# A hybrid-attention layer: the order of the first stage (loads, first products, squares of x) is changed

## The chip, the core and the metric

The kernel runs on one core of a Trainium2 chip. The metric is the time of one launch on the device, in microseconds, as the median of several runs. The engines are TensorE (PE in the profile; PEld is its weight load), VectorE (DVE), ScalarE (ACT), GpSimd (POOL) and SyncE (SP), which here only issues transfers. An engine takes its instructions in the order of the program, and waits at the first one whose inputs are not there.

## The reference

One decoder layer on 512 tokens of width 1024, all in float32:

```
h    = rms_norm(x, norm_in)
proj = h @ w_in                         # queries, keys, values and gates of two attention groups
a    = sliding-window attention with sinks (8 query heads, 2 key/value heads)
b    = block-sparse attention (8 heads, blocks of 256 keys)
x    = x + concat(a * silu(a_g), b * silu(b_g)) @ w_out
gate = sigmoid(rms_norm(x, ple_norm) @ w_ple_gate)
x    = x + (p @ w_ple_proj) * gate      # p: 512 x 256, w_ple_proj: 256 x 1024
out  = rms_norm(x, final_norm)
```

What matters here is the start: the product of p with w_ple_proj, the squares of x for the first norm, and the first projection (keys and values of the window group, "akv"), for which the normed x has to be transposed.

## The kernel before

Float32 operands are split in two parts, a rounded copy (the hi part, made by ACT, `AF.Copy`) and the rest (the lo part, made by DVE, `tensor_sub`). A product is then three products: hi by hi, lo by hi, hi by lo. `split_T` (L143, L144), `Weights.split` (L116, L118) and `split_ple` write such pairs.

The first stage is one block of the program, written by hand under `manual_schedule()`: every engine and every queue takes its instructions in the order in which the lines stand. It has these parts.

- **Loads.** p comes in four blocks of 128 tokens (`p_sb`), w_ple_proj in two halves of 512 columns with two row blocks each (`wraw_p[:, n, k]`), then x in four blocks (`x_t`), then the weights of akv. Before, SP's queue carries p, x and the second half of w_ple_proj, and ACT's queue the first half and `g_rows` (norm_in, 4 KB). A transfer takes one of eight completion semaphores in turn and waits for the transfer that had it before.
- **Dummy products** (`warm_up(n)`, L193): n products of a block of zeros, with no reader. 21 stand ahead of the first real work and 5 behind the first transposes.
- **p by w_ple_proj.** `p_trans(t)` (L245 to L247) transposes block t of p on PE into PSUM (two transposes), ACT writes the hi part (`pTh`) and DVE the lo part (`pTl`). `ple_mm(t, n, k)` (L283) is three products of 512 columns: hi by hi, lo by hi (`pTl`), hi by lo (`wpl`). There are four blocks t, two halves n and two row blocks k: 48 products. `ple_out` copies a finished bank to SBUF, on ACT ("A") or DVE ("D").
- **Squares and norms of x.** `x_square(t)` makes the sum of squares of block t, block 0 on DVE (L258), the others on ACT (L255); POOL makes the inverse root (L128, L133); `x_norm(t)` (L262, DVE) scales the block in place.
- **Transposes of x and akv.** `x_trans(k)` (L268, L270, L271) transposes column block k of all four blocks of x on PE, and ACT and DVE write the hi and lo parts, `acts`. `akv_mm(k)` (L302) is six products with them. Of the 48 products of p, the last six (block 3, second half) stand around the first transposes of x, before they begin and between the first two.

Everything behind (the projections of 16 weight chunks, both attentions, the output products) is left as it is. There the order comes from a list of pieces that are run between the steps of the attention.

Of the kernel before, what the change touches and what calls it, by code (L numbers as in the profile page):

```python
# [10 lines left out]
F32 = mybir.dt.float32  # L11
BF16 = mybir.dt.bfloat16
F32R = mybir.dt.float32r
AF = mybir.ActivationFunctionType
ALU = mybir.AluOpType

P = 128
# [21 lines left out]
def hybrid_layer_kernel(  # L39
# [130 lines left out]
    with ExitStack() as ph1:  # L170
# [4 lines left out]
        p_sb = cp1.tile([P, NT, PLE], F32, name="p_sb")  # L175
        pv = p.rearrange("l b (t p) d -> p (l b t) d", p=P)
        wraw_p = cp1.tile([P, 2, 2, 512], F32, name="wraw_p")
        nc.sync.dma_start(p_sb[:, 0:1], pv[:, 0:1])
        nc.scalar.dma_start(wraw_p[:, 0, 0], wp[:, 0, 0:512])
        nc.scalar.dma_start(wraw_p[:, 0, 1], wp[:, 1, 0:512])  # L180
        g_rows = cp1.tile([KC, P], F32, name="g_rows")
        nc.scalar.dma_start(g_rows, norm_in.rearrange("l (k c) -> (l k) c", c=P))
        nc.sync.dma_start(p_sb[:, 1:2], pv[:, 1:2])
        nc.sync.dma_start(p_sb[:, 2:4], pv[:, 2:4])
        warm = cp1.tile([P, P], BF16, name="warm")
        nc.vector.memset(warm, 0.0)
        first = cp1.tile([P, 1], F32, name="first")
# [3 lines left out]
        def warm_up(n):  # L191
            for _ in range(n):
                nc.tensor.matmul(accw[:, 0:P], warm[:, 0:P], warm, start=True, stop=True)  # L193
# [2 lines left out]
        g_col = cp1.tile([P, KC], F32, name="g_col")  # L196
        x_sb = [xp.tile([P, D], F32, name="x_t", bufs=NT) for t in range(NT)]
        nc.sync.dma_start(x_sb[0], x2d[0])
        nc.sync.dma_start(wraw_p[:, 1], wp[:, :, 512:1024])
        for t in range(1, NT):  # L200
            nc.sync.dma_start(x_sb[t], x2d[t])
# [59 lines left out]
        def x_norm(t):  # L261
            nc.vector.tensor_scalar_mul(x_sb[t], x_sb[t], rx[t])  # L262
# [17 lines left out]
        def ple_mm(t, n, k, parts=(0, 1, 2)):  # L280

            for j in parts:
                nc.tensor.matmul(pacc[t, n], (pTl if j == 1 else pTh)[:, k, tok(t)],  # L283
                                 (wpl if j == 2 else wph)[:, n, k], start=k == 0 and j == 0, stop=k == 1 and j == 2)
# [8 lines left out]
        def split_ple(n, k):  # L293
            split_T(wph[:, n, k], wpl[:, n, k], wraw_p[:, n, k])
# [10 lines left out]

        lo0 = p_trans(0)
        gp = bank([P, KC], "gp", "o")
        warm_up(5)
        for t in range(NT):
            ple_bank(t, 0)  # L310
        lo0()
        nc.scalar.activation(wph[:, 0, 0], wraw_p[:, 0, 0], AF.Copy)
        p_trans(1)()
        nc.vector.tensor_sub(wpl[:, 0, 0], wraw_p[:, 0, 0], wph[:, 0, 0].bitcast(F32))
        ple_mm(0, 0, 0, (0, 1))
        lo2, lo3 = p_trans(2), p_trans(3)
        nc.tensor.transpose(gp, g_rows, ident[0:KC, 0:KC])
        ple_mm(1, 0, 0, (0, 1))
        ple_mm(0, 0, 0, (2,))
        ple_mm(1, 0, 0, (2,))  # L320
        lo2()
        lo3()
        split_ple(0, 1)
        ple_mm(2, 0, 0)
        ple_mm(3, 0, 0)
        nc.vector.tensor_copy(g_col, gp)
        for t in range(NT):
            ple_mm(t, 0, 1)
        x_square(0, "D")
        split_ple(1, 0)  # L330
        x_norm(0)
        split_ple(1, 1)
        ple_out(0, 0, "A")
        ple_out(1, 0, "D")
        for t in range(3):
            ple_bank(t, 1)
            for k in range(2):
                ple_mm(t, 1, k)
        x_square(1)
        ple_out(2, 0, "D")  # L340
        ple_out(3, 0, "A")
        x_norm(1)
        x_square(2)
        x_norm(2)
        x_square(3)
        x_norm(3)
        ple_bank(3, 1)
        ple_mm(3, 1, 0)
        for m in range(2):
            akv[m] = bank([P, 512], "acc_akv", "S")  # L350
        x_trans(0)
        w_akv.split()
        tables = bias_tables()
        ple_mm(3, 1, 1)
        x_trans(1)
        w_akv.split()
        akv_mm(0)
        ple_out(0, 1, "D")
        ple_out(1, 1, "A")
# [631 lines left out]
```

## Time and profile before

| what | us |
|---|---|
| median of 3 runs | 323.25 (322.18 to 323.43) |
| the profiled execution | 322.3 |
| its span, first to last instruction | 320.6 |
| PE busy | 307.7 (96%) |
| DVE busy | 226.0 (70%) |
| ACT busy | 185.9 (58%) |
| POOL busy | 66.3 (21%) |

The page gives the busy time of each engine over the span; the view by stretches of time gives the same for parts of it. The timeline lists instructions with their start and length, and in brackets how long the engine had nothing to do before and what released it. The chain of waits follows the end back to the start. The profile page gives the granted clock of PE as full (9 of tenths) in all slices but the last one.

### The profile page before, as it was taken

To read this page: it belongs to the slowest core of one execution; us is meant where nothing else is said; L and a number is where in the kernel's file an instruction comes from. 1 tells how busy PE (TensorE), PEld (TensorE's weight loads), DVE (VectorE), ACT (ScalarE), POOL (GpSimd) and SP (SyncE) were. 2 spreads that over 40 slices of the span, in tenths; PEclk is the share of its full clock that TensorE was granted. 3 is DMA by queue.
4 is the path that set the end of the run, shared out by engine and by line. 5 is a ranking of instruction groups with operands and counts; after the bars stand their busy time and mean duration, and the time that the engine had idled before them with its cause. 6 is when DMAs were issued, how large, how long until landed. Compare 5 with 4: busy or idle time off the path is not lost.

```text
span 320.6 us, 4721 instructions
## 1 busy us (share of the span) xinstructions
PE 307.7 (96%) x1641; PEld 259.9 (81%) x1641; DVE 226.0 (70%) x516; ACT 185.9 (58%) x419; POOL 66.3 (21%) x118
## 2 busy tenths in 40 slices
PE   7999999999999999899999999999999999999990
PEld 6878788888889888699888878877888888888890
DVE  2876766886787868878878796859758656672544
ACT  4755656656475648677678676788157323541341
POOL 1240102435434351600003130012300110000011
PEclk9999999999999999999999999999999999999997
DMA  7962598150405072751443403004956700000113
GB/s 234 390 164 83 148 227 232 41 133 1 127 7 177 23 183 76 200 155 40 135 98 120 112 0 133 1 0 116 384 174 246 264 1 0 2 0 0 66 67 131
DMA packets 33224, 37.61 MB, mean 117 GB/s; under 512 B 1432, under 2 KB 24992, under 8 KB 33200
## 3 DMA queue, kind: packets, MB, share of 16 engines
q1 hardware_dynamic: 31952, 33.94, 34.0%
q0 software_dynamic: 800, 2.62, 4.2%
q10 hardware_dynamic: 448, 0.74, 0.7%
q8 instruction: 13, 0.21, 0.3%
q14 instruction: 11, 0.09, 0.1%
HBM read 32.52 MB, written 2.16 MB: 108 GB/s over the span
## 4 chain that ended last, share of the span: by engine, by line
PE 72%; DVE 12%; issue 6%; ACT 4%; POOL 3%; DMA 1%; POOLq 0%; SPq 0%; ACTq 0%; DVEq 0%
PE acc L451 8%; PE acc L452 8%; PE acc L453 8%; PE acc L137 7%; PE acc L139 7%; PE acc L138 7%; PE acc_ple L283 3%; PE acc_akv L302 3%; PE Sb L611 3%; PE accv L137 2%; PE oaccb L641 2%; PE accv L139 2%; PE accv L138 2%; PE tpb L631 2%; DVE q L499 2%
## 5 line engine op out<-in xcount | busy, mean ns | idle before, releaser
L557 ACT ACTIVATE st<-st,nm 128x257 f32<-128x257 f32 (+1 forms) x32 | 15.2, 478 | 22.0 <-DVE nm L554 20.0
L137 PE MATMUL acc<-hi_wg,h 128*128 128x512 f32 (+1 forms) x72 | 26.7, 370 | 0.0
L139 PE MATMUL acc<-hi_wg,h 128*128 128x512 f32 (+1 forms) x72 | 26.4, 367 | 0.0
L451 PE MATMUL acc<-acts,hi_bkq 128*128 128x512 f32 x64 | 26.4, 412 | 0.0
L138 PE MATMUL acc<-lo_wg,h 128*128 128x512 f32 (+1 forms) x72 | 26.3, 365 | 0.0
L451 PE MATMUL acc<-acts,hi_aqg 128*128 128x512 f32 x64 | 26.2, 410 | 0.0
L137 PE MATMUL acc<-hi_wo,acts 128*128 128x512 f32 x64 | 25.4, 397 | 0.5 <-DVE G L529 0.5
L453 PE MATMUL acc<-acts,lo_aqg 128*128 128x512 f32 x64 | 25.2, 393 | 0.0
L453 PE MATMUL acc<-acts,lo_bkq 128*128 128x512 f32 x64 | 25.1, 392 | 0.0
L139 PE MATMUL acc<-hi_wo,acts 128*128 128x512 f32 x64 | 25.1, 392 | 0.0
L452 PE MATMUL acc<-acts,hi_bkq 128*128 128x512 f32 x64 | 25.1, 392 | 0.0
L138 PE MATMUL acc<-lo_wo,acts 128*128 128x512 f32 x64 | 25.1, 392 | 0.0
L452 PE MATMUL acc<-acts,hi_aqg 128*128 128x512 f32 x64 | 25.1, 392 | 0.0
L614 ACT ACTIVATE stb<-stb,nmb 128x128 f32<-128x128 f32 (+3 forms) x32 | 17.8, 558 | 9.0 <-DVE nmb L612 8.7
L582 POOL TENSOR_SCALAR_AFFINE_SELECT pta<-pta 128x512 fp32r<-128x512 f32 x24 | 17.3, 719 | 14.3 <-DVE pta L144 13.2
L137 PE MATMUL accv<-hi_bv,acts 128*128 128x256 f32 x64 | 18.7, 293 | 1.5 <-DVE kt L144 1.5
L536 POOL TENSOR_TENSOR O<-O,sg 128x512 f32<-128x512 f32 x8 | 11.4, 1428 | 39.5 <-DVE sg L535 39.3
L139 PE MATMUL accv<-hi_bv,acts 128*128 128x256 f32 x64 | 18.0, 282 | 0.0
L138 PE MATMUL accv<-lo_bv,acts 128*128 128x256 f32 x64 | 18.0, 281 | 0.0
L839 ACT ACTIVATE sq<-x 128x512 f32<-128x512 f32 x15 | 9.5, 631 | 14.2 <-DVE x L901 11.6
L612 DVE CUSTOM_DVE_ANT_0 stb<-Sb,b_b 128x128 f32<-128x128 f32 (+3 forms) x32 | 15.5, 485 | 2.4 <-PE Sb L611 2.3
L508 POOL DMA_DIRECT2D kt<-kt x10 | 5.6, 563 | 51.1 <-DVE kt L144 48.7
(167 smaller groups left out, 872.6 us busy)
## 6 DMA issues: line engine op xcount, KB each, us to landing
raw_aqg<-in_w_in_dram SPq DMA_DIRECT2D x8, 512.0 KB, 5.3
raw_bkq<-in_w_in_dram SPq DMA_DIRECT2D x8, 512.0 KB, 4.6
raw_wo<-in_w_out_dram SPq DMA_DIRECT2D x4, 1024.0 KB, 6.3
raw_wg<-in_w_ple_gate_dram SPq DMA_DIRECT2D x4, 1024.0 KB, 5.0
kt<-kt POOLq DMA_DIRECT2D x10, 256.0 KB, 4.0
x_t<-in_x_dram SPq DMA_DIRECT2D x4, 512.0 KB, 7.4
raw_bv<-in_w_in_dram SPq DMA_DIRECT2D x2, 1024.0 KB, 5.4
b_b<-d_tab SPq DMA_DIRECT2D x8, 256.0 KB, 4.6
```

The source lines that it names most:

```text
L137: nc.tensor.matmul(acc, sh, mh, start=first, stop=False)
L138: nc.tensor.matmul(acc, sh, ml, start=False, stop=False)
L139: nc.tensor.matmul(acc, sl, mh, start=False, stop=last)
L283: nc.tensor.matmul(pacc[t, n], (pTl if j == 1 else pTh)[:, k, tok(t)], (wpl if j == 2 else wph)[:, n, k], start=k == 0 and j == 0, stop=k ...
L451: nc.tensor.matmul(acc, w.hi[:, k, cs], acts[:, k, 0, :], start=k == 0, stop=False)
L452: nc.tensor.matmul(acc, w.hi[:, k, cs], acts[:, k, 1, :], start=False, stop=False)
L453: nc.tensor.matmul(acc, w.lo[:, k, cs], acts[:, k, 0, :], start=False, stop=k == KC - 1)
L536: nc.gpsimd.tensor_mul(O[c], O[c], sg)
L557: nc.scalar.activation(st[:, s, lo_k:257], st[:, s, lo_k:257], AF.Exp, bias=nm[:, s:s + 1], scale=-1.0, accum_out=sm[:, s:s + 1])
L582: nc.gpsimd.affine_select(out=pt[:, :, b, :].rearrange("p j (s q) -> p j s q", s=2), in_=pt[:, :, 1, :].rearrange("p j (s q) -> p j s q", ...
L612: nc.vector.tensor_tensor_reduce(st[:, :w], S[:, :w], bias[:, 512 - w:], -1.0, 1.0e38, ALU.add, ALU.min, nm)
L614: nc.scalar.activation(st[:, :w], st[:, :w], AF.Exp, bias=nm, scale=-1.0, accum_out=sm)
```

## The change

The change is in the first stage alone.

- **Loads.** All go to SP's queue: first block of p, first row block of w_ple_proj, the other three blocks of p in one transfer, second row block, first block of x, `g_rows`, second half of w_ple_proj, the rest of x, akv.
- **Dummy products.** 9 in place of 5 behind the first transposes, and two further groups of 3: one between the first block's second and third product, one ahead of the second block's first product.
- **Products of p.** A block's three products stand together; the transposes of blocks 1 and 2 come behind the first block's products, those of block 3 behind the second block's. The transpose of `g_rows` comes behind all first products.
- **Squares and copies.** The three squares on ACT stand one behind the other, with no copy between them; the copy of the first bank goes from ACT to DVE. The square of block 0 on DVE stands behind the split of the second row block, as before, and the copy of `g_col` behind one more split.
- **akv.** The first two splits of the akv weights come ahead of the first transposes of x, and the last six products of p stand behind the first and behind the second group of transposes of x.

```diff
--- before.py
+++ after.py
@@ -175,13 +175,11 @@
         p_sb = cp1.tile([P, NT, PLE], F32, name="p_sb")
         pv = p.rearrange("l b (t p) d -> p (l b t) d", p=P)
         wraw_p = cp1.tile([P, 2, 2, 512], F32, name="wraw_p")
+        g_rows = cp1.tile([KC, P], F32, name="g_rows")
         nc.sync.dma_start(p_sb[:, 0:1], pv[:, 0:1])
-        nc.scalar.dma_start(wraw_p[:, 0, 0], wp[:, 0, 0:512])
-        nc.scalar.dma_start(wraw_p[:, 0, 1], wp[:, 1, 0:512])
-        g_rows = cp1.tile([KC, P], F32, name="g_rows")
-        nc.scalar.dma_start(g_rows, norm_in.rearrange("l (k c) -> (l k) c", c=P))
-        nc.sync.dma_start(p_sb[:, 1:2], pv[:, 1:2])
-        nc.sync.dma_start(p_sb[:, 2:4], pv[:, 2:4])
+        nc.sync.dma_start(wraw_p[:, 0, 0], wp[:, 0, 0:512])
+        nc.sync.dma_start(p_sb[:, 1:4], pv[:, 1:4])
+        nc.sync.dma_start(wraw_p[:, 0, 1], wp[:, 1, 0:512])
         warm = cp1.tile([P, P], BF16, name="warm")
         nc.vector.memset(warm, 0.0)
         first = cp1.tile([P, 1], F32, name="first")
@@ -196,6 +194,7 @@
         g_col = cp1.tile([P, KC], F32, name="g_col")
         x_sb = [xp.tile([P, D], F32, name="x_t", bufs=NT) for t in range(NT)]
         nc.sync.dma_start(x_sb[0], x2d[0])
+        nc.sync.dma_start(g_rows, norm_in.rearrange("l (k c) -> (l k) c", c=P))
         nc.sync.dma_start(wraw_p[:, 1], wp[:, :, 512:1024])
         for t in range(1, NT):
             nc.sync.dma_start(x_sb[t], x2d[t])
@@ -305,55 +304,56 @@
 
         lo0 = p_trans(0)
         gp = bank([P, KC], "gp", "o")
-        warm_up(5)
+        warm_up(9)
         for t in range(NT):
             ple_bank(t, 0)
         lo0()
-        nc.scalar.activation(wph[:, 0, 0], wraw_p[:, 0, 0], AF.Copy)
+        split_ple(0, 0)
+        ple_mm(0, 0, 0, (0, 1))
+        warm_up(3)
+        ple_mm(0, 0, 0, (2,))
         p_trans(1)()
-        nc.vector.tensor_sub(wpl[:, 0, 0], wraw_p[:, 0, 0], wph[:, 0, 0].bitcast(F32))
-        ple_mm(0, 0, 0, (0, 1))
-        lo2, lo3 = p_trans(2), p_trans(3)
-        nc.tensor.transpose(gp, g_rows, ident[0:KC, 0:KC])
-        ple_mm(1, 0, 0, (0, 1))
-        ple_mm(0, 0, 0, (2,))
-        ple_mm(1, 0, 0, (2,))
+        lo2 = p_trans(2)
+        warm_up(3)
+        ple_mm(1, 0, 0)
         lo2()
+        lo3 = p_trans(3)
+        ple_mm(2, 0, 0)
         lo3()
         split_ple(0, 1)
-        ple_mm(2, 0, 0)
         ple_mm(3, 0, 0)
-        nc.vector.tensor_copy(g_col, gp)
+        nc.tensor.transpose(gp, g_rows, ident[0:KC, 0:KC])
         for t in range(NT):
             ple_mm(t, 0, 1)
         x_square(0, "D")
         split_ple(1, 0)
+        nc.vector.tensor_copy(g_col, gp)
+        split_ple(1, 1)
+        x_square(1)
         x_norm(0)
-        split_ple(1, 1)
-        ple_out(0, 0, "A")
+        ple_out(0, 0, "D")
         ple_out(1, 0, "D")
+        x_square(2)
+        x_norm(1)
         for t in range(3):
             ple_bank(t, 1)
             for k in range(2):
                 ple_mm(t, 1, k)
-        x_square(1)
+        x_square(3)
         ple_out(2, 0, "D")
+        x_norm(2)
         ple_out(3, 0, "A")
-        x_norm(1)
-        x_square(2)
-        x_norm(2)
-        x_square(3)
         x_norm(3)
         ple_bank(3, 1)
-        ple_mm(3, 1, 0)
+        w_akv.split()
+        w_akv.split()
         for m in range(2):
             akv[m] = bank([P, 512], "acc_akv", "S")
         x_trans(0)
-        w_akv.split()
+        ple_mm(3, 1, 0)
+        x_trans(1)
+        ple_mm(3, 1, 1)
         tables = bias_tables()
-        ple_mm(3, 1, 1)
-        x_trans(1)
-        w_akv.split()
         akv_mm(0)
         ple_out(0, 1, "D")
         ple_out(1, 1, "A")
```

PE at the first products, before. `acc_ple_174` to `_177` are the banks of blocks 0 to 3 of p, `tp_188` and `tp_192` the transposes of blocks 2 and 3, `wph`/`wpl` the hi and lo parts of w_ple_proj:

```order
L283 MATMUL acc_ple_174<-wph_160,pTh_162 128x512
L283 MATMUL acc_ple_174<-wph_160,pTl_163 128x512
L245 MATMUL tp_188<-ident_77,p_sb_93 128x128 x2
L245 MATMUL tp_192<-ident_77,p_sb_93 128x128 x2
L317 MATMUL gp_168<-ident_77,g_rows_98 128x8
L283 MATMUL acc_ple_175<-wph_160,pTh_162 128x512
L283 MATMUL acc_ple_175<-wph_160,pTl_163 128x512
L283 MATMUL acc_ple_174<-wpl_161,pTh_162 128x512
L283 MATMUL acc_ple_175<-wpl_161,pTh_162 128x512
```

The same place now. The banks are `_177` to `_180`, `tp_190` and `tp_195` are the transposes of blocks 1 and 2, and the rows of L191 are a dummy product's weight load and product (two more pairs follow them):

```order
L282 MATMUL acc_ple_177<-wpl_160,pTh_161 128x512
L244 MATMUL tp_190<-ident_77,p_sb_93 128x128 x2
L244 MATMUL tp_195<-ident_77,p_sb_93 128x128 x2
L191 LDWEIGHTS warm_100
L191 MATMUL accw_104<-warm_100 128x128
```

The transposes of block 1, which before stood ahead of the first product, and those of block 2 now stand behind the third product of block 0; the hi and lo parts of block 1, on which the fourth product waits, are made only after that.

DVE from the split of the second row block (first row) to the last scaling of x, before. `x_t_129` to `_132` are the four blocks of x, `acc_ple_175` and `_176` the banks of blocks 1 and 2:

```order
L144 TENSOR_TENSOR wpl_161<-wraw_p_94,wph_160 128x512
L326 COPY g_col_128<-gp_168 128x8
L258 ISA sqD_224,ssq_225<-x_t_129,epst_80 128x1024
L258 ISA ssq_225 128x1
L144 TENSOR_TENSOR wpl_161<-wraw_p_94,wph_160 128x512
L262 TENSOR_SCALAR x_t_129<-x_t_129,rs3_227 128x1024
L144 TENSOR_TENSOR wpl_161<-wraw_p_94,wph_160 128x512
L291 COPY ple_84<-acc_ple_175 128x512
L291 COPY ple_84<-acc_ple_176 128x512
L262 TENSOR_SCALAR x_t_130<-x_t_130,rs3_262 128x1024
L262 TENSOR_SCALAR x_t_131<-x_t_131,rs3_272 128x1024
L262 TENSOR_SCALAR x_t_132<-x_t_132,rs3_280 128x1024
```

The same stretch now, from the square of block 0 on, with the blocks of x as `x_t_127` to `_130`:

```order
L257 ISA sqD_232,ssq_233<-x_t_127,epst_80 128x1024
L144 TENSOR_TENSOR wpl_160<-wraw_p_94,wph_159 128x512
L330 COPY g_col_126<-gp_167 128x8
L144 TENSOR_TENSOR wpl_160<-wraw_p_94,wph_159 128x512
L261 TENSOR_SCALAR x_t_127<-x_t_127,rs3_235 128x1024
L290 COPY ple_84<-acc_ple_177 128x512
L290 COPY ple_84<-acc_ple_178 128x512
L261 TENSOR_SCALAR x_t_128<-x_t_128,rs3_247 128x1024
L290 COPY ple_84<-acc_ple_179 128x512
L261 TENSOR_SCALAR x_t_129<-x_t_129,rs3_257 128x1024
L261 TENSOR_SCALAR x_t_130<-x_t_130,rs3_286 128x1024
L118 TENSOR_TENSOR lo_akv_294<-raw_akv_137,hi_akv_293 128x512 x2
```

DVE has one copy more between the square of block 0 and the last scaling, and two splits of akv right behind it.

ACT from the splits of w_ple_proj on, before:

```order
L143 ACTIVATE wph_160<-wraw_p_94 128x512 x3
L289 ACTIVATE ple_84<-acc_ple_174 128x512
L255 ACTIVATE sqA_257,ssq_258<-x_t_130 128x1024
L289 ACTIVATE ple_84<-acc_ple_177 128x512
L255 ACTIVATE sqA_267,ssq_268<-x_t_131 128x1024
L255 ACTIVATE sqA_275,ssq_276<-x_t_132 128x1024
L270 ACTIVATE acts_83<-tpx_289,g_col_128 128x512
L116 ACTIVATE hi_akv_296<-raw_akv_138 128x512
```

And now:

```order
L143 ACTIVATE wph_159<-wraw_p_94 128x512 x3
L254 ACTIVATE sqA_242,ssq_243<-x_t_128 128x1024
L254 ACTIVATE sqA_252,ssq_253<-x_t_129 128x1024
L254 ACTIVATE sqA_281,ssq_282<-x_t_130 128x1024
L288 ACTIVATE ple_84<-acc_ple_180 128x512
L116 ACTIVATE hi_akv_293<-raw_akv_137 128x512 x2
L269 ACTIVATE acts_83<-tpx_301,g_col_126 128x512
```

The squares no longer stand behind copies that wait for PE, and the first parts of the akv weights are made ahead of the first `acts`.

## Rows read from the trace of the kernel before

**Rows 1.** The page: busy time, its share of the span, instructions.

```profile
PE 307.7 (96%) x1641; PEld 259.9 (81%) x1641; DVE 226.0 (70%) x516; ACT 185.9 (58%) x419; POOL 66.3 (21%) x118
```

**Rows 2.** Stretches of time: busy (instructions) by engine, PE clock, DMA share, GB/s.

```profile
8.00:18.20 10.20, 10.20 (x44) 8.44 (x44) 7.77 (x14) 6.37 (x12) 3.44 (x7) 1.00 1.07 376
18.20:35.00 16.80, 16.49 (x86) 12.96 (x85) 11.37 (x19) 11.55 (x21) 2.45 (x8) 1.00 0.40 103
35.00:100.00 65.00, 64.40 (x363) 55.31 (x362) 50.35 (x142) 38.11 (x101) 22.54 (x37) 1.00 0.41 107
```

**Rows 3.** Timeline of PE to 18.0 us: start, length, instruction, idle before.

```profile
3.99 0.66 PE L245 MATMUL tp<-ident,p_sb 128*128 128x128 f32 x2 [0.52 <-DMA p_sb<-in_p_dram]
...
5.80 0.77 PE L283 MATMUL acc_ple<-wph,pTh 128*128 128x512 f32 x1
6.37 0.63 PE L283 MATMUL acc_ple<-wph,pTl 128*128 128x512 f32 x1
6.80 1.06 PE L245 MATMUL tp<-ident,p_sb 128*128 128x128 f32 x4
...
8.92 0.62 PE L283 MATMUL acc_ple<-wpl,pTh 128*128 128x512 f32 x2
...
10.76 0.39 PE L283 MATMUL acc_ple<-wph,pTh 128*128 128x512 f32 x1
...
18.01 0.39 PE L283 MATMUL acc_ple<-wpl,pTh 128*128 128x512 f32 x1
```

**Rows 4.** Timeline of ACT: first weight split, hi parts of p, last square of x.

```profile
4.97 0.62 ACT L312 ACTIVATE wph<-wraw_p 128x512 fp32r<-128x512 f32 x1
...
7.46 0.81 ACT L246 ACTIVATE pTh<-tp 128x256 fp32r<-128x256 f32 x2 [0.90 <-PE tp L245]
...
15.35 1.06 ACT L255 ACTIVATE sqA<-x_t 128x1024 f32<-128x1024 f32 x1
```

**Rows 5.** Timeline of DVE, 7.9 to 18.4 us.

```profile
7.88 0.85 DVE L247 TENSOR_TENSOR pTl<-tp,pTh 128x256 fp32r<-128x256 f32 x2 [0.26 <-ACT pTh L246]
...
9.44 0.16 DVE L326 COPY g_col<-gp 128x8 f32<-128x8 f32 x1
9.51 1.28 DVE L258 CUSTOM_DVE_ANT_0 sqD<-x_t,epst 128x1024 f32<-128x1024 f32 x1
...
11.85 0.75 DVE L262 TENSOR_SCALAR x_t<-x_t,rs 128x1024 f32<-128x1024 f32 x1 [0.45 <-POOL rs L133]
12.52 0.68 DVE L144 TENSOR_TENSOR wpl<-wraw_p,wph 128x512 fp32r<-128x512 f32 x1
13.12 1.28 DVE L291 COPY ple<-acc_ple 128x512 f32<-128x512 f32 x2
...
17.70 0.75 DVE L262 TENSOR_SCALAR x_t<-x_t,rs 128x1024 f32<-128x1024 f32 x1 [0.71 <-POOL rs L133]
```

**Rows 6.** Timeline of PE around the first transposes of x.

```profile
18.24 0.60 PE L268 MATMUL tpx<-ident,x_t 128*128 128x128 f32 x4
18.60 0.48 PE L283 MATMUL acc_ple<-wph,pTh 128*128 128x512 f32 x1
...
22.09 0.60 PE L268 MATMUL tpx<-ident,x_t 128*128 128x128 f32 x4
...
23.91 0.60 PE L268 MATMUL tpx<-ident,x_t 128*128 128x128 f32 x4
```

**Rows 7.** The microsecond from 3.00, columns as in the second group.

```profile
3.00:4.00 1.00, 0.48 (x6) 0.24 (x3) 0.00 (x0) 0.82 (x2) 0.00 (x0) 1.00 1.04 385
```

**Rows 8.** By line: first row block of w_ple_proj, last three blocks of x, to landing.

```profile
L179 ACTq DMA_DIRECT2D wraw_p<-in_w_ple_proj_dram x1: 410/410/410, 0.8 to 0.8; - x1
DMA to landing us min/median/max: 3.5/3.5/3.5
L201 SPq DMA_DIRECT2D x_t<-in_x_dram x3: 328/598/682, 4.3 to 5.4; - x3
DMA to landing us min/median/max: 6.9/7.8/8.4
```

## The prediction

> **What bounds the kernel now.** I read the page first: PE is busy 96% of the span, DVE 70%, ACT 58% [rows 1]. A change that adds no real product can then only remove time in which PE has nothing to do or runs slowly, 320.6 - 307.7 = 12.9 us in the whole span. The stretches of time come next: from 35 us on PE is busy 64.40 of 65.00 us, and from 8.0 to 18.2 us without a break [rows 2]. What the first stage can still give lies ahead of 8 us and around 18 to 22 us. So I went through the timeline of PE there.
>
> Ahead of 8 us PE waits for the first block of p, whose transposes start at 3.99 us [rows 3], then for the hi part of the weights, made by ACT from 4.97 to 5.59 us [rows 4]; the first product stands at 5.80 us [rows 3]. It is slow as well: the second product begins at 6.37 and PE goes on at 6.80, so 512 columns take 0.43 us, while the 32 products between the 13th (10.76) and the 45th (18.01) take 7.25 us, 0.227 us each [rows 3]. These are the two levels, 1.2 and 2.4 GHz; the step lies near 8.9 us, behind stretches in which PE had work, then gaps, then work almost without a gap. The granted clock of the stretches reads 1.00 throughout [rows 2], so the spacing of the products tells the step and that column does not.
>
> At 18 to 22 us the transposes of x begin twice, at 18.24 and 22.09, 3.85 us apart [rows 6]. Work between them: four transposes (18.60 - 18.24 = 0.36), three products (0.68), four transposes and six akv products (one round, 23.91 - 22.09 = 1.82) [rows 6]. That is 2.86 us, so some 1.0 us is waiting there.
>
> **The change, part by part.** The sum goes to the point where the third group of transposes of x starts (22.09 before), since behind it both programs have the same work.
>
> The first products. The first two stay at 5.80 and 6.37, as the hi part of the weights ends at 5.59 as before. Then come three dummy products, each a quarter of 0.43 us, so 0.3 us, and the third product (0.43): PE is at 7.55. Only now the transposes of blocks 1 and 2 are issued. Before, the hi part began 0.66 us behind the start of such transposes (7.46 against 6.80) and the lo part 0.42 us behind the hi part [rows 3 to 5]. So block 1's hi part begins at 8.2, its lo part runs from 8.63 to 9.05, and the fifth product waits for that. Block 3's transposes follow the sixth product at about 9.55; at full rate its hi part starts at 10.1, its lo part ends at 10.9, products 10 to 12 end at about 11.4, and the 13th starts at 11.5, where it was 10.76: 0.75 us later, if the rate rises at 8.9 us as now. The second group of three and the nine cost nothing, since they stand where PE waits for ACT or DVE. The first group of three does not: the lo weights are there at 5.59 + 0.68, some 6.3, and PE is free at 6.80, so its 0.3 us is paid, and is in this sum.
>
> From the 13th product, 30 more stand ahead of the transposes of x (33 before): 30 x 0.227 = 6.8, so PE is there at 18.3 (18.24 before).
>
> DVE. It must make the lo parts of the second weight block (10.9 to 11.55) before the square of block 0, and then has one copy more. From the square to the last scaling, by rows 5: square 1.28, split 0.60 (13.12 - 12.52), copy of `g_col` 0.07 (9.51 - 9.44), split 0.60, scaling 0.67 (12.52 - 11.85), two copies 1.28, scaling 0.67, copy 0.64, scaling 0.67, last scaling 0.75: 7.2 us, so the last scaling ends at 18.75 (18.45 before). ACT's squares do not bind: the last began at 15.35 [rows 4] although its block had landed at 5.4 + 8.4 = 13.8 [rows 8], and back to back behind the splits the three go on from 12.1 and end by 15.7.
>
> Around the transposes. The fourth transpose follows the last scaling, so the first group ends at 18.85. Then three products 0.68, transposes 0.36, three products 0.68, six akv products 1.46: the third group starts at 22.03, against 22.09. The waiting of 1.0 us is covered by the moved products and by the akv weights, which are split at 18.75 to 20.0 on DVE while PE works; the lo part of the first `acts` follows until 20.75, and the second akv product wants it at 20.8. So what this place gives (0.8), the start takes back: -0.06 us.
>
> The queue. Before, the first row block of the weights was issued from ACT at the same 0.8 us as the first block of p, and landed 3.5 us later, at 4.3 [rows 8]; p was there at 3.99. Issued behind it on one queue, it moves 262 KB less beside p. At worst p lands as now: 0. At best the half of the moved bytes that lay ahead of p's end, 131 KB at 385 GB/s [rows 7], are gone: 0.34 us, for the whole chain. I take half, 0.17. SP issues one transfer more ahead of x; x itself comes no sooner, as the transfers are busy throughout (share 1.07 from 8.0 to 18.2 us [rows 2]) and the bytes are the same. The Trainium skill, page DMA: Bandwidth & Descriptors, section "Issuing engines are not separate DMA queues", says that transfers of all issuing engines run on the same 16 DMA engines and interleave, and that several issuing engines save only the issue time. By that rule the first block, alone on the engines, would have the whole 0.34; the other side, that the one queue costs ACT's parallel issue (some 0.4 us for the first weights), is hidden behind the 0.7 us between their landing and their use.
>
> The clock. If the filled gaps make the rate rise earlier, at about 6 us, products and transposes from the third on halve, and the chain to the 13th product shortens by about 1.1 us: the third product 0.2, dummies 0.3, transposes 0.3, the start of the next blocks 0.3. DVE's chain starts earlier by the same. The trace shows one rise and cannot bound this: 0 to 1.1, and down to -0.5 if it comes a microsecond later, as ten half-rate products would move 0.2 each but mostly into waits. I take a quarter, 0.28, as the gap before the first transposes stays. The row that speaks for more is the stretch of 5.8 to 8.9 itself, where the rate rose behind nearly closed work.
>
> Sum: -0.06 - 0.17 - 0.28 = -0.5 us. Everything behind 22 us is products back to back, so the shift is carried to the end. The profiled execution took 322.3 us, 0.95 below the median of the three runs and inside their spread; the four are 322.8 on average, and I set the forecast on that: 322.3 us.
>
> **The rivals.** First, the rate rises early. For it: dummies in two further places, and 9 in place of 5. Against it: the idle 0.52 us ahead of the first transposes [rows 3] is untouched. Gain 0.06 + 0.1 + 1.1 = 1.25 us, time 321.5. The Trainium skill, page TensorE: Matmul & The Clock Gate, section "Part 1: The HAM clock gate", says that the throttled rate is the default and that sustained work of the engine releases it; by that rule dummy products as such bring the rise forward, which is this rival.
>
> Second, the other side: DVE becomes the bound. If its chain runs by the full lengths of rows 5 (three scalings 0.08 longer, splits 0.68, `g_col` 0.16: 7.75 us) and starts at 11.6, the last scaling ends at 19.35, the two akv splits at 20.7 and the first lo part of `acts` at 21.45, and the third group starts at 22.8: 0.7 slower, about 323.6. It decides from a square of block 0 that starts later than 11.3 us. For it: the order puts everything behind one engine. Against it: DVE starts such operations before the last has ended.
>
> Third, the change does not do what it says: the dummies lie beside waits that remain, p lands at 3.99, and the start gives back what the end gains. Time 322.8.
>
> **How the numbers follow.** Forecast 0.45, early rise 0.25, nothing 0.17, DVE 0.13. About 0.5%, 1.6 us, is what a measurement of this kernel can tell from no change; faster means under 321.6, slower over 324.9. Faster needs most of the early rise, on top of runs as low as the profiled one: half of its 0.25 and a sixth of the forecast's 0.45, 0.20. Slower needs DVE's case and more: 0.05. Runs of before spread over 1.25 us, and the cases reach from -1.25 to +0.8: I take 320.9 to 324.0.
>
> **What would show it.** Right: first transposes at 3.65 to 3.99; the 13th product between 10.9 and 11.5; the last scaling at 17.9 to 18.75; no wait for the akv weights near 20 us; the third group of transposes near 21.5. Early rise: products 0.23 apart before 8 us and the third group at 20.9. DVE: PE idle ahead of the first transposes of x, with the last scaling as releaser. Wrong: a later wait at 20 to 35 us that takes the gain back, or a transfer of p that lands after 7.5 us.

## The result and the profile after

The changed kernel takes 321.19 us, the median of eight runs (320.88 to 321.55). The kernel before, timed beside it on the same chip, takes 323.18 us, the median of eight (322.18 to 324.53). The ratio is 0.9934, with a 95% interval of 0.9916 to 0.9953: faster by 2.0 us, some 0.6 us to each side. The spread fell as well, from 2.35 to 0.67 us. The profiled executions lie closer together, 322.3 us (span 320.6) and 321.41 us (span 319.7): the one of before lies near the low end of its range.

The forecast was 322.3 us; 321.19 lies in its range, but it is the time of the rival "the rate rises early" (321.5 us), which had a chance of 0.25. It is also below 321.6 us, to which the prediction gave a chance of 0.20.

The page's busy times changed little. PE has ten dummies more:

```profile
PE 307.7 (96%) x1651; PEld 259.8 (81%) x1651; DVE 226.3 (71%) x517; ACT 185.6 (58%) x418; POOL 66.6 (21%) x118
```

So the gain is in time in which nothing ran, or ran slowly, as [rows 1] allowed: span minus busy time of PE falls from 12.9 to 12.0 us. The timeline of PE (start, length, instruction, idle before and its releaser) shows where; the rows answer to [rows 3] and [rows 6]:

```profile
1.04 2.42 PE L191 MATMUL accw<-warm 128*128 128x128 bf16 x21 [1.04 <-DVE warm L184]
3.26 0.64 PE L244 MATMUL tp<-ident,p_sb 128*128 128x128 f32 x2
3.69 1.17 PE L191 MATMUL accw<-warm 128*128 128x128 bf16 x9
4.89 0.80 PE L282 MATMUL acc_ple<-wph,pTh 128*128 128x512 f32 x1
5.48 0.63 PE L282 MATMUL acc_ple<-wph,pTl 128*128 128x512 f32 x1
5.91 0.41 PE L191 MATMUL accw<-warm 128*128 128x128 bf16 x3
6.14 0.48 PE L282 MATMUL acc_ple<-wpl,pTh 128*128 128x512 f32 x1
...
10.46 0.50 PE L282 MATMUL acc_ple<-wph,pTh 128*128 128x512 f32 x1
...
17.41 0.60 PE L267 MATMUL tpx<-ident,x_t 128*128 128x128 f32 x4
...
19.69 0.62 PE L301 MATMUL acc_akv<-acts,hi_akv 128*128 128x512 f32 x2
...
21.07 0.60 PE L267 MATMUL tpx<-ident,x_t 128*128 128x128 f32 x4
```

Read beside before: the first transposes come at 3.26 (3.99), with no idle time ahead of them, right behind the 21 dummies; the first product at 4.89 (5.80); the step in rate near 6.0 (8.9), since the three dummies at 5.91 take 0.23 us until the next instruction and the product ahead of them takes 0.43; the 13th product at 10.46 (10.76); the first transposes of x at 17.41 (18.24); the akv products behind the second group at 19.69 with no wait; the third group at 21.07 (22.09). That lead of 1.02 us stays (the first product behind the akv stage starts at 34.12 us, before at 35.15): the stretch behind it (busy, instructions by engine, clock, DMA share, GB/s) has no gap, where [rows 2] had 0.31 us of them.

```profile
17.40:34.00 16.60, 16.60 (x89) 13.55 (x88) 11.14 (x18) 11.01 (x21) 1.99 (x8) 1.00 0.46 118
```

The first block of p landed 2.1 us after its issue, where before it was 3.1 (issue at 0.80, use at 3.99). Between 2 and 3 us the DMA engines moved more than twice as much, but over the first 4 us both kernels moved the same (135 and 132 GB/s). First the two rows of after, then those of before, same columns:

```profile
2.00:3.00 1.00, 1.00 (x12) 1.00 (x11) 0.00 (x0) 0.27 (x2) 0.31 (x2) 1.00 0.87 277
0.00:4.00 4.00, 2.96 (x26) 2.90 (x27) 0.11 (x1) 1.55 (x3) 1.52 (x12) 1.00 0.47 135
```

```profile
2.00:3.00 1.00, 1.00 (x12) 1.00 (x11) 0.00 (x0) 0.67 (x1) 0.30 (x2) 1.00 0.47 126
0.00:4.00 4.00, 2.43 (x22) 2.20 (x22) 0.11 (x1) 1.49 (x2) 1.51 (x12) 1.00 0.42 132
```

The queues of before up to 3.0 us (packets, MB, share of the engines; q1 is SP's, q10 ACT's):

```profile
q1 hardware_dynamic: 101, 0.10, 17.7%
q10 hardware_dynamic: 19, 0.04, 3.3%
```

So p, which comes first on SP's queue, was slow before ACT's queue had moved much beside it.

DVE at the square of block 0 and at the last two scalings (columns as for PE) answers to [rows 5]; between them it has no wait either:

```profile
10.30 1.28 DVE L257 CUSTOM_DVE_ANT_0 sqD<-x_t,epst 128x1024 f32<-128x1024 f32 x1
...
15.90 1.41 DVE L261 TENSOR_SCALAR x_t<-x_t,rs 128x1024 f32<-128x1024 f32 x2
```

And ACT, where the last square ([rows 4]: 15.35) and the akv splits now wait for transfers alone:

```profile
13.66 1.06 ACT L254 ACTIVATE sqA<-x_t 128x1024 f32<-128x1024 f32 x1 [0.15 <-DMA x_t<-in_x_dram]
16.60 1.16 ACT L116 ACTIVATE hi_akv<-raw_akv 128x512 fp32r<-128x512 f32 x2 [1.30 <-DMA raw_akv<-in_w_in_dram]
```

### The profile page after: what moved, and what is told of

Its sections match the earlier page's. It is cut to its first block, busy times and chain, and to the rows that moved or that the text cites. A ratio compares the mean times of both kernels' runs of the same rounds, so it can differ in the third digit from the quotient of the medians.

```text
span 319.7 us, 4741 instructions
## 1 busy us (share of the span) xinstructions
PE 307.7 (96%) x1651; PEld 259.8 (81%) x1651; DVE 226.3 (71%) x517; ACT 185.6 (58%) x418; POOL 66.6 (21%) x118
## 4 chain that ended last, share of the span: by engine, by line
PE 73%; DVE 12%; issue 6%; ACT 4%; POOL 3%; POOLq 0%; DVEq 0%; ACTq 0%
PE acc L451 8%; PE acc L452 8%; PE acc L453 8%; PE acc L137 7%; PE acc L139 7%; PE acc L138 7%; PE acc_ple L282 4%; PE acc_akv L301 4%; PE Sb L611 3%; PE accv L137 2%; PE oaccb L641 2%; PE accv L139 2%; PE accv L138 2%; PE tpb L631 2%; DVE q L499 2%
```

## The experiments

Three causes compete, and they can add up. The rate: PE is kept at work across the arrival of p, so that its full rate comes earlier. The late half: the order behind the products of the first weight block (squares back to back, akv split early, three more products between the transposes). The queue: p is simply earlier by a microsecond. In each pair, "before" is the kernel before in the same job on the same chip; the medians of before differ by up to 0.4 us from job to job, so kernels are compared inside a job. The timelines have the columns of [rows 3].

### One half at a time: the queue, the order, the dummies, the late half

These four shared one chip with 34 runs of before (median 322.98 us, 321.82 to 324.23).

**The queue alone**: before, with the loads of after.

```diff
 nc.sync.dma_start(p_sb[:, 0:1], pv[:, 0:1])
-nc.scalar.dma_start(wraw_p[:, 0, 0], wp[:, 0, 0:512])
-nc.scalar.dma_start(wraw_p[:, 0, 1], wp[:, 1, 0:512])
-nc.scalar.dma_start(g_rows, ...)
-nc.sync.dma_start(p_sb[:, 1:2], pv[:, 1:2])
-nc.sync.dma_start(p_sb[:, 2:4], pv[:, 2:4])
+nc.sync.dma_start(wraw_p[:, 0, 0], wp[:, 0, 0:512])
+nc.sync.dma_start(p_sb[:, 1:4], pv[:, 1:4])
+nc.sync.dma_start(wraw_p[:, 0, 1], wp[:, 1, 0:512])
...
 nc.sync.dma_start(x_sb[0], x2d[0])
+nc.sync.dma_start(g_rows, ...)
```

> The kernel before with the loads of the changed one (one queue, order of use), nothing else. Queue theory (the earlier landing of p's first block, 2.9 in place of 3.9 us, is what moves the start): first transposes at 3.3 us as in the changed kernel, but the order of before wants block 1's transposes ahead of the first product, and their transfer lands at 6.0, so the first product comes near 6.2 and the time stays at 323.2 within 0.4: the queue pays only with the new order. Dummy theory (the gain is the earlier rise of PE's rate): no dummies added, 323.2. Late theory (the gain is the covered wait at 18 to 22 us): 323.2.

Measured: 324.08 us (322.96 to 325.79), ratio 1.0037 [1.0015, 1.0058]: slower. Its timeline of PE:

```profile
3.26 0.63 PE L244 MATMUL tp<-ident,p_sb 128*128 128x128 f32 x2
5.68 0.69 PE L244 MATMUL tp<-ident,p_sb 128*128 128x128 f32 x2 [1.26 <-DMA p_sb<-in_p_dram]
6.03 0.77 PE L282 MATMUL acc_ple<-wph,pTh 128*128 128x512 f32 x1
...
12.11 0.44 PE L282 MATMUL acc_ple<-wph,pTl 128*128 128x512 f32 x1
12.38 0.39 PE L282 MATMUL acc_ple<-wpl,pTh 128*128 128x512 f32 x1
```

The first block is as early as in the changed kernel, and nothing comes of it. In the old order the transposes of block 1 stand ahead of the first product, and block 1 now comes in the transfer of three blocks, behind the weights: PE waits 1.26 us for it, and the rate rises only near 12.2 (the first of the last two products above takes 0.27 us, the next ones 0.23, those before them 0.43).

**The queue undone**: after, with the loads of before (the diff above the other way round).

> The changed kernel with the loads of before (p and x on SP's queue, first weights and g_rows on ACT's). Queue theory: p's first block lands at 3.9 again, first transposes at 3.99, everything up to the first transposes of x 0.6 to 0.9 us later, time 321.9. Dummy theory: 321.2 to 321.4, as the rate still rises by about 6 us. Late theory: 321.2.

Measured: 323.19 us (322.58 to 324.14), ratio 1.0003 [0.9985, 1.0020]: the new order, with all its dummies, gains nothing on two queues. PE:

```profile
4.60 0.66 PE L245 MATMUL tp<-ident,p_sb 128*128 128x128 f32 x2 [1.13 <-DMA p_sb<-in_p_dram]
6.25 0.80 PE L283 MATMUL acc_ple<-wph,pTh 128*128 128x512 f32 x1
...
10.94 0.48 PE L283 MATMUL acc_ple<-wph,pTh 128*128 128x512 f32 x1
11.26 0.40 PE L283 MATMUL acc_ple<-wph,pTl 128*128 128x512 f32 x1
```

In this execution, the slowest of the twelve (324.14 us), p landed 3.7 us after its issue, PE had nothing to do for 1.13 us, and the step in rate came near 10.9 (0.32 us to the next product, 0.23 from there on). So queue and order each gain nothing alone, and 0.66% together.

**Without the new dummies**: after with 5 in place of 9 and without the two groups of 3.

```diff
-warm_up(9)
+warm_up(5)
...
-warm_up(3)
```

> The changed kernel with 5 dummy products behind the first transposes as before and without the two groups of 3. Dummy theory: the rise of PE's rate goes back from 6.1 to about 8.9 us, the 13th product comes 0.5 to 1 us later, time 321.8 to 322.2, and the runs spread by 1 us or more as those of before do. Queue theory and late theory: 321.2, or 0.1 to 0.2 less, since the first group of 3 stood where PE did not wait.

Measured: 321.20 us (320.86 to 322.26), ratio 0.9945 [0.9926, 0.9964]. The median is that of the changed kernel in its own job (321.19 us), and the intervals of the two ratios overlap; the upper end of the range lies higher. Its profiled execution (322.02 us) lies near that end:

```profile
5.06 0.79 PE L282 MATMUL acc_ple<-wph,pTh 128*128 128x512 f32 x1 [0.64 <-ACT wph L143]
...
8.66 0.49 PE L282 MATMUL acc_ple<-wpl,pTh 128*128 128x512 f32 x1
...
11.11 0.50 PE L282 MATMUL acc_ple<-wph,pTh 128*128 128x512 f32 x1
```

The step comes near 8.7 here, about where it is in [rows 3]: the case that the prediction's sum was worked out for. The additional dummies are thus not what made the kernel faster. Whether they narrow its spread is not shown: it is 1.40 us over eleven runs here and 0.67 us over eight of the changed kernel, but 1.20 us over six runs of a version below that has all of them (the small transfer on ACT's queue).

**The late half alone**: before, with everything behind the products of the first weight block as in after (the lower part of the diff from `x_square(0, "D")` on).

> The kernel before with the second half of the change alone: squares back to back, first copy on DVE, akv weights split ahead of the first transposes of x, last six products of p behind the transposes. Late theory: from the first to the third group of transposes of x only work remains, the 1.0 us of waiting goes, time 322.2. Queue theory and dummy theory: the start is as before, and they expect at most half of it, 322.7 or more.

Measured: 322.43 us (321.44 to 323.58), ratio 0.9988 [0.9966, 1.0011]: at best half of the gain, and not apart from none. The profiled execution was its slowest; p came late (4.54), and the step near 12.4:

```profile
4.54 0.66 PE L245 MATMUL tp<-ident,p_sb 128*128 128x128 f32 x2 [1.08 <-DMA p_sb<-in_p_dram]
...
19.70 0.60 PE L268 MATMUL tpx<-ident,x_t 128*128 128x128 f32 x4
...
23.36 0.60 PE L268 MATMUL tpx<-ident,x_t 128*128 128x128 f32 x4
```

From 19.70 to 23.36 it works as in the changed kernel (3.66 us, no wait), but in this execution the start has lost more than that (19.70 against 18.24 in [rows 6]).

### What p waits for, and what the kernel before does in other runs

These four shared another chip with 17 runs of before (median 323.33 us, 322.15 to 324.67).

**The kernel before once more**, unchanged, to see an execution other than the one of the rows.

> The kernel before, unchanged, for a second profile: its runs spread over 2.4 us (321.8 to 324.2) where those of the changed one spread over 0.7. Landing theory (with two queues p's first block lands anywhere from 3.9 to 4.6 us, and PE's rate rises anywhere from 8.7 to 12.4 us, and that makes the spread): first transposes between 3.9 and 4.6 us, and the first product of the akv-to-query change-over later than 35.15 by as much as the profiled time is above 322.3. Rival (the spread arises later in the kernel): the first stage as in the first profile, 35.15 within 0.2, whatever the time.

Measured: 321.58 us.

```profile
3.98 0.63 PE L245 MATMUL tp<-ident,p_sb 128*128 128x128 f32 x2 [0.51 <-DMA p_sb<-in_p_dram]
4.43 0.46 PE L193 MATMUL accw<-warm 128*128 128x128 bf16 x5
...
9.89 0.39 PE L283 MATMUL acc_ple<-wph,pTh 128*128 128x512 f32 x1
...
21.32 0.60 PE L268 MATMUL tpx<-ident,x_t 128*128 128x128 f32 x4
```

The same program, the same landing of p (3.98 against 3.99 in [rows 3]), the same 0.51 us without work: here the step came near 4.4, not at 8.9: five dummies take 0.46 us in this run and 0.74 at the low rate, in the execution of the rows:

```profile
4.45 0.74 PE L193 MATMUL accw<-warm 128*128 128x128 bf16 x5
```

The third group of transposes is at 21.32 in place of 22.09, 0.77 us earlier, the first product behind the akv stage is at 34.38 in place of 35.15, also 0.77 us earlier, and the time is 0.72 us less. So the difference arises in the first stage, the price of a late rise can be read from two executions of one program, and its moment is not fixed by the program alone. The landing theory had the place of the spread right and its reason in part: p landed no sooner here, and the rate rose 4.5 us sooner.

**The queue alone, p in two transfers**: the wait that made the queue alone slower, taken away in part.

```diff
-nc.sync.dma_start(p_sb[:, 1:4], pv[:, 1:4])
+nc.sync.dma_start(p_sb[:, 1:2], pv[:, 1:2])
+nc.sync.dma_start(p_sb[:, 2:4], pv[:, 2:4])
```

> The kernel before with the one queue, but blocks 1 to 3 of p in two transfers as before (block 1, then 2 and 3). Order theory (q_alone was slower only because the old order wants block 1 ahead of the first product and it came with a transfer of three blocks, landing at 5.7): block 1 lands near 4.3, the first product stands at about 5, time 321.8 to 322.4. Rival (one queue makes the old order slow by itself, by a late rise of PE's rate): 323.0 or more, with the rise near 12 us as in q_alone.

Measured: 325.00 us (322.71 to 326.20), ratio 1.0038 [1.0010, 1.0066], with runs around 323 and around 325.5. The one profiled is of the first kind (323.29 us):

```profile
4.83 0.44 PE L245 MATMUL tp<-ident,p_sb 128*128 128x128 f32 x2 [0.69 <-DMA p_sb<-in_p_dram]
...
8.18 0.22 PE L317 MATMUL gp<-ident,g_rows 8*128 8x8 f32 x1 [1.49 <-DMA g_rows<-in_norm_in_dram]
```

Block 1 is no longer the wait, the next one is: the transpose of `g_rows` stands third among PE's tasks, and on the one queue `g_rows` lies behind x's first block. It costs 1.49 us. That is what the change's order takes out of the way, by putting this transpose behind all first products. The rate is not what holds this execution back: its five dummies at 3.69 take 0.45 us, so the step came near 3.7, the earliest of all. The time is the rival's, its reason is not. What made the runs around 325.5 was not profiled.

**A small transfer on ACT's queue**: after, with `g_rows` (4 KB) issued there at the start.

```diff
 nc.sync.dma_start(p_sb[:, 0:1], pv[:, 0:1])
+nc.scalar.dma_start(g_rows, ...)
...
-nc.sync.dma_start(g_rows, ...)
```

> The changed kernel with one difference: the 4 KB of g_rows are issued from ACT's queue at the very start. Queue theory A (a second queue in use at the start delays p by itself): p's first block lands at 3.6 us or later, time 322 or more. Queue theory B (it is the 512 KB of weights that shared the engines with p): p lands at 2.7 to 2.9 as in the changed kernel, time 321.2 within 0.2.

Measured: 321.22 us (321.07 to 322.27), ratio 0.9938 [0.9914, 0.9962]. p's first block lands 2.1 us after its issue, as in the changed kernel:

```profile
L179 SPq DMA_DIRECT2D p_sb<-in_p_dram x1: 381/381/381, 0.8 to 0.8; - x1
DMA to landing us min/median/max: 2.1/2.1/2.1
```

A second queue that carries 4 KB does not delay p. What is left is that the slower landing goes with large transfers on both: 524 KB of weights on ACT's queue and the other blocks of p directly behind the first on SP's. Which of the two counts for more was not taken apart, and that they share the engines with p, as theory B has it, is not shown: up to 3.0 us ACT's queue had moved 0.04 MB in the kernel before.

**A version meant to be better**: after, with 18 dummies in place of 21, no dummies between the products of block 0, the second row block split one step earlier, and one copy moved back to ACT.

```diff
-warm_up(21)
+warm_up(18)
...
-ple_mm(0, 0, 0, (0, 1))
-warm_up(3)
-ple_mm(0, 0, 0, (2,))
+ple_mm(0, 0, 0)
...
 lo2()
+split_ple(0, 1)
 lo3 = p_trans(3)
 ple_mm(2, 0, 0)
 lo3()
-split_ple(0, 1)
+ple_mm(0, 0, 1)
 ple_mm(3, 0, 0)
...
-ple_out(2, 0, "D")
+ple_out(2, 0, "A")
```

> A version that should beat both: the changed kernel with 18 dummies at the start, no dummies between block 0's second and third product, the split of the second weight block and block 0's products with it moved ahead of block 3's, and the copy of bank 2 on ACT. If the start of DVE's chain (square of block 0 at 10.3, last scaling at 17.3) and the 1.4 us in which PE waits between 7 and 10.5 us bound the changed kernel: square of block 0 near 9.6, transposes of x at 16.9, time 320.7. If the first transposes of x are bound by x's landing (13.6 us) and the akv weights (16.6): 321.1. If the missing dummies let the rate rise late: 321.3 and a spread over 1 us.

Measured: 320.97 us (320.75 to 321.23), ratio 0.9923 [0.9903, 0.9943], the lowest time of all kernels here; its interval overlaps that of the changed kernel, so a gain over it of some 0.2 us is not shown. The first transposes moved up to 3.08 us, and DVE has time to spare now: its last scaling ends at 16.85, and PE goes from its products into the transposes of x at 17.11 without a wait. So neither DVE nor the landing of x holds PE there. The square of block 0 came at 9.48 and the time lies between the two forecasts.

```profile
17.11 0.60 PE L267 MATMUL tpx<-ident,x_t 128*128 128x128 f32 x4
```

### The gap closed by dummies alone, and the late half undone

What was open: whether the gap ahead of the first transposes is the cause, or only goes with it. These four shared a third chip with 28 runs of before (median 322.89 us, 321.91 to 324.47).

**Before with more dummies**: 30 at the start, so that they last until p is there on two queues, and 9 behind the first transposes. Loads and order are those of before.

```diff
-warm_up(21)
+warm_up(30)
...
-warm_up(5)
+warm_up(9)
```

> The kernel before with more dummy products and nothing else: 30 at the start in place of 21 (they end near 4.15 us, about when p's first block lands) and 9 behind the first transposes in place of 5. Rate theory (the 2.0 us between the medians are mostly PE's rate, which in most runs of before rises at 8.7 us or later and in the changed kernel near 6): first transposes at 4.2 to 4.6, the rise near 6 us or earlier in most runs, time 321.6 to 322.2, spread below 1.2 us. Landing theory (p's later landing by itself, and the order, make the gap): 322.8 to 323.3, with the spread of before, 2.4 us.

Measured: 321.69 us (321.46 to 321.82), ratio 0.9955 [0.9940, 0.9970]: 1.2 us less in the median, and a spread of 0.36 us where before has 2.56.

```profile
4.22 0.53 PE L245 MATMUL tp<-ident,p_sb 128*128 128x128 f32 x2
4.59 0.67 PE L193 MATMUL accw<-warm 128*128 128x128 bf16 x9
5.75 0.49 PE L283 MATMUL acc_ple<-wph,pTh 128*128 128x512 f32 x1
...
9.85 0.39 PE L283 MATMUL acc_ple<-wph,pTh 128*128 128x512 f32 x1
...
21.13 0.60 PE L268 MATMUL tpx<-ident,x_t 128*128 128x128 f32 x4
```

The first transposes are later than before (4.22 against 3.99), no real work is added, taken away or moved, and yet the third group of transposes comes 0.96 us earlier than in [rows 6]. The nine dummies at 4.59 take 0.67 us, where they take 1.17 at the low rate. What changed is the rate. Both groups of dummies were made longer together here; in the next run the nine stand on both sides, and only 30 for 21 is new.

**The same on the new order with two queues**: the kernel with the queue undone, and 30 dummies at the start.

> The changed kernel with the two queues of before (323.19 with 21 dummies at the start) and 30 dummies at the start in place of 21. Rate theory: the one queue pays because p lands while PE is still busy with dummies, so that the rate rises early; with the gap closed by dummies the time is 321.6 to 322.0. Landing theory: the first transposes stay at 4.2 to 4.6 in place of 3.3 and the time at 322.6 or more.

Measured: 321.89 us (321.56 to 322.50), ratio 0.9972 [0.9957, 0.9987], where without the additional dummies it had 1.0003.

```profile
5.58 0.50 PE L283 MATMUL acc_ple<-wph,pTh 128*128 128x512 f32 x1 [0.49 <-ACT wph L143]
```

Closing the gap gives back some 1 us here too. The rest to the changed kernel, 0.8 us in this job, goes with the later p: the first transposes at 4.18 and the first product at 5.58, there at 3.26 and 4.89.

**The late half undone**: after, with everything behind the products of the first weight block as before.

> The changed kernel with the second half of before: squares of x between copies, first copy on ACT, akv weights split behind the first transposes of x, last six products ahead of and between the transposes. Late theory: the waiting of some 1.0 us between the first and the third group of transposes of x is back, time 322.0 to 322.2. Rival (the late part costs DVE what it gives PE): 321.2 to 321.5.

Measured: 322.19 us (321.89 to 322.81), ratio 0.9976 [0.9963, 0.9989]. The first product stands at 4.89 and the step in rate is early (near 4.8):

```profile
17.59 0.81 PE L267 MATMUL tpx<-ident,x_t 128*128 128x128 f32 x4
...
19.70 0.77 PE L301 MATMUL acc_akv<-acts,hi_akv 128*128 128x512 f32 x2 [0.16 <-ACT hi_akv L116]
...
21.64 0.60 PE L267 MATMUL tpx<-ident,x_t 128*128 128x128 f32 x4
```

Its last scaling of x waits 0.44 us for its factor and ends at 18.01, and the akv products wait for their weights: 4.05 us from the first to the third group, where [rows 6] have 3.85 for the same order.

**The changed kernel once more**, unchanged, beside these.

> The changed kernel, unchanged, for a second profile and for its median on this chip beside the others. Both theories: 321.0 to 321.4, spread below 1 us, first transposes at 3.26, the rise between 4.5 and 7 us.

Measured: 321.07 us (320.99 to 321.73), ratio 0.9949 [0.9928, 0.9971].

```profile
4.89 0.50 PE L282 MATMUL acc_ple<-wph,pTh 128*128 128x512 f32 x1
...
9.96 0.50 PE L282 MATMUL acc_ple<-wph,pTh 128*128 128x512 f32 x1
...
20.69 0.60 PE L267 MATMUL tpx<-ident,x_t 128*128 128x128 f32 x4
```

With the step at 4.8 in both executions, the late half is worth 21.64 - 20.69 = 0.95 us in the traces and 322.19 - 321.07 = 1.12 us in the medians.

This job gives a chain of medians from the kernel before to the changed one: 322.89, the gap closed 321.69 (-1.20), with that the queue, the new first order and its own dummies in place of the old start 322.19 (+0.50), and the late half 321.07 (-1.12). The runs of neighbours in this chain do not overlap (321.91 to 324.47, 321.46 to 321.82, 321.89 to 322.81, 320.99 to 321.73). The middle step is a loss. The traces show it too: the new start has its first product 0.86 us earlier (4.89 against 5.75) and its 13th 0.11 us later (9.96 against 9.85), both at an early full rate. What more it loses comes by way of the norms of x: the square of block 0 starts at 9.80 against 9.03, and the last scaling, for which the last of the first transposes of x waits, ends at 18.01 against 17.55; the third group of transposes is 0.51 us later (21.64 against 21.13). With the gap closed either way, the old first order is at least as good. The kernel that this chain points to, before with 30 dummies and the late half, was not run; if the steps add up, an estimate is 321.69 - 1.12 = 320.6 us.

## Why the prediction was right or wrong

**The case.** The likeliest case was not the one that came. The forecast held the rise of the rate near where it was and took a quarter of 1.1 us for an earlier one. In the profiled execution it came 2.9 us earlier, at 6.0, and the places are then those of the rival: the 13th product forecast at 11.5 - 1.1 = 10.4, measured 10.46; the third group of transposes forecast at 20.9, measured 21.07; the time 321.5, measured 321.41 in that execution and 321.19 in the median.

**The step that failed first** is "the gap before the first transposes stays". It rested on the landing of p, the term of 0 to 0.34 us of which 0.17 was taken. Measured: the landing 1.0 us sooner, the transposes 0.73 us sooner, the first product 0.91 us sooner. The term counted the bytes that move ahead of p at 385 GB/s, the rate of the microsecond from 3.00 [rows 7]. But most of p travels before that, and there the engines moved 126 GB/s in the kernel before and 277 in the changed one. The same 131 KB at 126 GB/s give 1.04 us, but that would be the right number for a reason that is not shown: up to 3.0 us ACT's queue had moved only 0.04 of 0.14 MB in the kernel before. That p lands sooner is shown; what slows it beside the second queue is open. With p at 2.9 us the 21 dummies, which end at about 3.4, reach beyond it, and the gap of 0.52 us, named as the reason against an early rise, was gone. The Trainium skill (DMA: Bandwidth & Descriptors, "Issuing engines are not separate DMA queues") says that transfers of all issuing engines run on the same DMA engines and interleave. The runs agree in direction, as p in front on one queue lands sooner; the gain was three times the 0.34 us that the prediction drew from it.

**The baseline** was the second thing too low. One trace shows one moment for the rise, and the sum was made against it. The moment varies: 4.4 us in one run of the kernel before, 8.9 in another, 10.9 and 12.4 in two kernels that share its queues and in which p happened to land late. The Trainium skill (TensorE: Matmul & The Clock Gate, "Part 1: The HAM clock gate") says that under sustained work the moment varies by some 500 ns from run to run. The runs agree that it varies and show more: 4.0 to 6.7 us in the seven executions without a gap that the last section lists. The median of 323.2 probably holds many late rises, as dummies alone take 1.2 us from it (an execution of before as slow as its median was not profiled), and a change that makes them early gains more than any one trace shows: 2.0 us in the medians, 0.9 between the two profiled executions. That runs of before spread over 1.25 us was in the prediction, but as noise around the forecast and not as something that the change could remove.

**The clock's rival** had the right mechanism, and the additional dummies for it were the wrong reason: without them the median is the same within the noise (321.20). The work that keeps PE busy across the arrival of p was there before; p came too late for it. The Trainium skill (TensorE: Matmul & The Clock Gate, "Part 1: The HAM clock gate") says that sustained work releases the throttle; the runs agree, above all the kernel before with more dummies, -1.2 us for no real work.

**What held.** The loss at the start was there, and larger than forecast. From the first to the 13th product the prediction had 5.7 us for 4.96 [rows 3], 0.3 of it the first group of dummies; the run without that group and with the step near 8.7 took 11.11 - 5.06 = 6.05. That the 13th product came at the rival's place (10.46 for 10.4) is in part luck: p's earlier landing, which that case did not have, offset the dearer order, and a second execution of the same kernel had it at 9.96. The late part: a gain of 0.8 us forecast, 0.95 in the traces and 1.1 in the medians. DVE's chain from the square to the last scaling: 7.2 us forecast, 17.31 - 10.30 = 7.0 measured, back to back. The rival "DVE becomes the bound" did not come, since the square began at 10.30 and its condition was 11.3. The wait for the akv weights near 20 us is gone, and x did not come sooner: ACT waited for its last block until 13.66, and it had landed at 13.8.

**Two misses that offset each other.** "What this place gives (0.8), the start takes back" was right in kind: in the chain of medians the start loses 0.50 us, although p comes a microsecond sooner, and the late half gains 1.12. The net is half a microsecond more than the 0.06 of the sum.

## What to carry to other kernels

When a first stage has stand-in work that keeps PE busy until the first load is there, compare the end of that work with the landing of that load, in several executions: a gap there, 0.5 to 1.1 us long, cost 1.2 us in the median here, and most of the spread between runs. Put nothing large on a second queue beside the transfer that everything waits for (here it landed 2.1 us after its issue in place of 3.1), and then order the consumers by the new order of landing: the one queue without the new order lost 0.4%, the new order without the queue gained nothing. And read the spread of the runs as a quantity that has a cause in the trace, before the median of a few is taken as the baseline.

## What was not expected of the hardware

- With large transfers on two queues at the start, the first 131 KB took 3.0 to 3.7 us to land (six executions), in place of 1.9 to 2.1 on one queue (eight). A second queue with a 4 KB transfer did not do it. From 2 to 3 us the engines moved 126 GB/s against 277, but over the first 4 us 132 against 135, so the bytes come through and only p is not ahead. Up to 3.0 us the second queue had moved 0.04 of 0.14 MB, so its bytes alone do not explain the slow start. What does stays open.
- The same program, with p landing at the same time (first transposes at 3.98 and 3.99 us), had the step to the full rate at 4.4 in one execution and at 8.9 in another. The granted clock of the stretches reads 1.00 in both; only the spacing of the products shows it (0.43 against 0.23 us for 512 columns).
- In all seven executions in which PE went without a gap from the first dummies through the transposes and the dummies behind them, and then waited at most 0.5 us ahead of the next product or transposes, the step lay between 4.0 and 6.7 us. With a gap of 1.1 us ahead of the transposes (two executions), or of 1.26 us behind them (one), it lay at 10.9 to 12.4. With a gap of 0.5 to 0.65 us at either place it lay at 4.4 in one execution and at 8.7 to 8.9 in two. In the last of the fourteen, the queue alone with p in two transfers, it lay at 3.7, ahead of a gap of 0.69 us. Up to that moment its PE had done what it did in the queue alone, where the step came at 12.2: closing the gap makes an early step likely here, and it does not fix the moment.
